# Moving sums of down-projection weights between stages, reordering the last up-projection's splits, and halving the last result's columns

## The chip, the cores and the metric

The kernel runs on one core of a Trainium2 chip. A core has a matrix engine (TensorE, PE in the profile, with its weight loads as PEld), a vector engine (VectorE, DVE), a scalar engine (ScalarE, ACT), a general engine (GpSimd, POOL), and a queue engine (SyncE, SP or SPq) that here issues nearly all transfers. The engines run their own instruction streams in order and wait for each other by semaphores. The metric is the device time of one execution in microseconds (us), as a median over runs.

## The reference, cut to what matters

One layer of a streaming encoder over a prompt of 2048 tokens and 8 short sequences of 16 tokens, in float32. Both go through the same layer with the same weights.

```python
def trunk_layer(x, ...):
    qm, km, vm, om, ip, fp, qa, ka, va = split_in(x @ w_in)
    hm = mlstm_chunkwise(qm, km, vm, logi, logf, C0, n0, m0, mchunk)
    hm = sigmoid(om) * head_norm(hm, g_mlstm_norm)
    ha = windowed attention of rope(qa), rope(ka), va with sinks
    mix = concatenate([hm, ha]) @ w_out
    h = layer_norm(DEEPNORM_ALPHA * x + mix, ln1_g, ln1_b)
    f, conv_rows = conv_ffn(h, conv_prev, w_up, w_conv, b_conv, w_down)
    y = layer_norm(DEEPNORM_ALPHA * h + f, ln2_g, ln2_b)

def conv_ffn(h, conv_prev, w_up, w_conv, b_conv, w_down):
    u = h @ w_up
    ext = concatenate([conv_prev, u], axis=1)
    c = b_conv + sum(ext[:, j:j + T] * w_conv[j] for j in range(CONV_W))
    a, g = split(c, 2)
    return (silu(g) * a) @ w_down, ext[:, -(CONV_W - 1):]
```

The model width is 1024, the input projection 2824 wide, the feed-forward width 2816 (the up-projection twice that, value and gate).

## The kernel before, in words

Tokens are in 17 tiles of 128 (16 of the prompt, one of the 8 short sequences). Three things explain most of the code.

First, every float32 matrix product is made of three products of rounded operands: an operand is split into a rounded high part and the rest (`split`, lines 215 to 218: ScalarE casts, VectorE subtracts), and high x high, high x low and low x high are added in the accumulator. Tiles `w`, `oh`/`ol`, `uw`, `hh`/`hl`, `fu` are such split operands; `wraw` holds the weights as loaded.

Second, each large product is done by seven smaller products instead of eight (Strassen's scheme in Winograd's form), which are numbered s = 1 to 7. They need sums and differences of quarters of the weights and of the tokens, and their results are added up while they are evicted from the accumulator banks A, B and C.

Third, TensorE's order is written by hand; the order on the other engines comes from a scheduler, which places each instruction by when it was issued in the program, its inputs and a few hints (`high_priority`, `issue_after`).

The stages, with their times in the profiled execution: the input projections in four blocks of tokens (b = 0 at 18 to 156 us, b = 1 at 168 to 292, b = 2 at 304 to 460, b = 3 at 472 to 628), woven with the chunkwise recurrence and the attention ("chains"); the output projection (634 to 914); the up-projection (914 to 1847) in three blocks of tokens and 22 column tiles j; the down-projection (1847 to 2312).

What the change touches:

- `i_dense` (line 587 on) walks through blocks b, column groups g (0 to 4; `last` is 4) and products s. Near its end (lines 682 to 687) it calls `d_sums`.
- `d_sums(k, step)` (840) prepares weights of the down-projection ahead of time: for each of 11 indices k it loads two weight tiles (`txy`, step 0, lines 844 and 845), makes four half-width sums on VectorE (step 1, lines 850 to 853) and stores both to `zt` (step 2, lines 855 and 856). The two `txy` tiles take the slots `xr1` and `xr3` that also hold raw tokens for the next block (`x_load`, line 537). Eight of the 11 are done in the input projections and three in the output projection (`o_block`, 1610).
- Gate rows: VectorE works out the logarithms of the gates (`gate_logs`, lines 980 to 997), TensorE multiplies them (`gate_rows`, 1006 and 1007, tile `pgr`).
- Head norm of the recurrence: statistics (1149, 1150), scaling (1152, 1155), small factors (1156 to 1166), scaling again (1168) and a transpose on TensorE (1178, tile `pht`). `ql`, `qh` are the split queries of the attention; `col` (1025) and `emt` (1030) are columns for the recurrence's exponentials.
- `f_ups` (1816): after every product it prepares later ones; with `left` products to go it calls `d_weights` (2009: load and split one unit of weights of the down-projection) and `d_tokens` (2027: split one unit of its tokens, tile `fu`, from `r`). `f_product` (1877) writes the banks; `f_evict` reads them; for s = 5, lines 1906 and 1908 add bank C to a copy of B. At the end `conv_p` and `conv_s` are stored. The last four products of the sequence are s = 5, 2, 3, 4 of the last column tile; s = 4 writes bank C again.
- `f_downs` (2056) runs the down-projection, three blocks, seven products each, six units u of weight rows, up to three token tiles p; line 2087 is its matmul, 512 columns wide. `after` and `add` (2112 to 2118) evict. The very last product is s = 3 of the last block, whose columns p run backwards and end with p = 0. `norm_last` (1540) and `stats` (1550) then do the last layer norm: `bn_stats` per 512 columns (1559), `bn_aggr` (1560), a power on GpSimd (1562), two passes in halves (1545, 1547) and the stores (1548). `st` holds the statistics of the last tile's left half, taken early.

Of the kernel before, what the change touches and what calls it, by code (L numbers as in the profile page):

```python
# [8 lines left out]
F32 = mybir.dt.float32  # L9
# [195 lines left out]
class Prog:  # L205
# [381 lines left out]
    def i_dense(self):  # L587
        nc, a = self.nc, self.a
        nb = len(IBLOCKS)
        last = NG - 1  # L590

        self.next_raw()
        self.x_load(0, 2)
        for _ in range(3):
            self.next_raw()
        self.x_load(0, 4)
        self.single_raw = self.tp.tile([P, KD, P], F32, name="xsr", tag="pth", bufs=2)
        nc.sync.dma_start(self.single_raw, a["xs"])
        self.angles = {}
        self.rope_load(IBLOCKS[0][2], 2)  # L600
        self.rope_load(NPT, 1)
        self.next_split()
        self.x_steps(0, "b12")
        for _ in range(3):
            self.next_split()
        self.x_steps(0, 3)
        self.x_single(1, 2)
        self.x_load(0, 1)
        self.next_raw()
        self.x_load(0, 3)  # L610
        self.x_steps(0, 1)
        self.advance()
        self.x_steps(0, 2, "t3", 7, "t2", 6)
        self.x_single(4)
        self.x_steps(0, "t1", 5, "t4")
        self.sb, self.trans = {}, None

        passages = [{1: ["load"], 7: ["t3", 7], 6: ["t2", 6], 3: [3, "t4"], 4: ["b12", "t1"]},
                    {1: ["load"], 6: ["t3"], 7: [7, "t2"], 5: [6], 3: [3, "t4"], 4: ["b12", "t1"]}]
        sums = 0  # L620
        after = None
        for item in self.items:
            if after:

                after[0] -= 1
                if after[0] == 3:
                    self.logs_of(after[1] - 1)
                if after[0] < 0:
                    self.i_done = after[1]
                    after = None  # L630
            self.chains.hold = item[0] == "t" and item[1] > 0
            if item[0] == "t":
                _, b, ti, e = item
                if ("g", e, 3) not in self.wu:
                    self.advance()
                if b not in self.gates:
                    self.gates[b] = self.tp.tile([P, 5, 8], F32, name="gates", tag="gates", bufs=2)
                ps = self.bank([P, 512], "pg") if ti == 4 else self.ib[ti % 2 * 2]
                yield from self.i_direct(b, ti, e, ps)
                self.i_keys(b, ti, ps)  # L640
                if ti == 1:
                    if b + 1 < nb:
                        self.x_steps(b + 1, 1, 2)
                    else:
                        self.release(4)
                    after = [6, b + 1]
                elif ti == 3 and b or ti == 4:
                    self.release(4)
                    self.x_steps(b, 4)
                    if b:  # L650
                        self.x_steps(b, 5)
                self.advance()
                continue
            _, b, g, s = item
            if item not in self.wu:
                self.advance()
            yield from self.i_product(b, g, s)
            del self.wu[item]
            self.release(2)
            if self.trans and s != 4:  # L660
                self.i_transposes()
            with self.tc.high_priority():
                behind = self.i_after(b, g, s)
            if (b, g, s) == (0, 0, 7):
                self.t_setup()
            if (g, s) == (1, 6):
                self.rope_load(IBLOCKS[b][0], 2)
            if g == last and b + 1 < nb:
                if s == 7:
                    self.rope_load(IBLOCKS[b + 1][2], 2)  # L670
                for x in passages[b > 0].get(s, ()):
                    if x == "load":
                        self.spare = True
                        self.x_load(b + 1, 1, 2, 3, 4)
                    else:
                        self.x_steps(b + 1, x)
            if g == last and b + 1 == nb and s in (7, 5, 2, 3):
                self.x_pair(0, (7, 5, 2, 3).index(s))
            with self.tc.issue_after(behind) if behind and b == 0 else nullcontext():
                self.advance()  # L680

            if b >= nb // 2 and g < last:

                steps = (6, 2, 5) if g == last - 1 else (6, 5, 3)
                if s in steps:
                    self.d_sums(sums, steps.index(s))
                    sums += s == steps[2]
        self.sums = sums
        self.logs_of(nb - 1)
        self.chains.hold = False  # L690
# [846 lines left out]
        self.mix_out(t, 4, mix)  # L1537


    def norm_last(self, y, g, bb, dst, st):  # L1540

        nc, V = self.nc, self.nc.vector
        mv, s = self.stats(y, st)
        for c in (slice(0, 512), slice(512, 1024)):
            V.scalar_tensor_tensor(y[:, c], y[:, c], mv[:, 0:1], g[:, c], op0=ALU.subtract, op1=ALU.mult)
        for c in (slice(0, 512), slice(512, 1024)):
            V.scalar_tensor_tensor(y[:, c], y[:, c], s[:, 0:1], bb[:, c], op0=ALU.mult, op1=ALU.add)
            nc.sync.dma_start(dst[:, c], y[:, c])

    def stats(self, y, st=None):  # L1550
        nc = self.nc
        V = nc.vector
        half = st is not None
        if not half:
            st = self.wp.tile([P, 2, 6], F32, name="lst", tag="lst", bufs=2)
        mv = self.wp.tile([P, 2], F32, name="lmv", tag="lmv", bufs=2)
        s = self.wp.tile([P, 2], F32, name="lsc", tag="lsc", bufs=2)
        for i in range(half, 2):
            V.bn_stats(st[:, i], y[:, i * 512:(i + 1) * 512])  # L1559
        V.bn_aggr(mv, st)  # L1560
        V.tensor_scalar_add(s[:, 1:2], mv[:, 1:2], EPS)
        nc.gpsimd.tensor_tensor(s[:, 0:1], s[:, 1:2], self.mhalf[:, 0:1], op=ALU.pow)
        return mv, s
# [252 lines left out]
    def f_ups(self, n):  # L1816
# [11 lines left out]
        for i, (b, j, s) in enumerate(self.seq):  # L1828
# [25 lines left out]
                self.d_begin()  # L1854

            left = len(self.seq) - i
            if left in (8, 7, 5, 3, 1):
                self.d_weights()
            if left in (9, 8, 7, 6):
                self.d_tokens()  # L1860
        nc.sync.dma_start(self.a["conv_p"], self.prev.rearrange("p v j r -> p (v j) r"))
        nc.sync.dma_start(self.a["conv_s"], self.convs.rearrange("p v j b r -> p (v j) b r"))

# [15 lines left out]
    def f_evict(self, b, j, s):  # L1879
# [22 lines left out]
        elif s == 5:  # L1902
            self.ug = u = half(1)
            u4 = f2.tile([P, 384], F32, name="ub", tag="ub", bufs=1)[:, :h]
            S.copy(u4, B)
            V.tensor_add(u[:, 2 + h:2 + WP], C[:, :m], u4[:, :m])
            if has_s:
                V.tensor_add(sam(u)[:, :, 2:], dec(C), dec(u4))  # L1908
        elif s == 3:
            S.copy(self.uv[:, 2 + h:2 + WP], B[:, :m])  # L1910
            if has_s:
                S.copy(sam(self.uv)[:, :, 2:], dec(B))
        elif s == 4:
            V.tensor_add(self.ug[:, 2:2 + h], C, self.u2[j % 2])  # L1914
# [141 lines left out]
    def f_downs(self):  # L2056
# [17 lines left out]
        nb, nu = len(FBLOCKS), len(DUNITS)  # L2074
        ys, ops = {}, {}
        last_tile = FBLOCKS[-1][0]
        st = self.wp.tile([P, 2, 6], F32, name="st", tag="st", bufs=1)

        def product(s, p, units):
            ps = banks[role[s][2 if p == np_ else p]]  # L2080
            c = slice(p * P, p * P + P)
            for u in units:
                wh, wl, fh, fl = ops[u]
                n = len(DUNITS[u])
                for k in range(n):
                    for i, (l, r) in enumerate(((fh, wh), (fh, wl), (fl, wh))):
                        mm(ps, l[:, k, c], r[:, k], start=s in (1, 4, 7) and u == 0 and k == 0 and i == 0,  # L2087
                           stop=u == nu - 1 and k == n - 1 and i == 2, skip_group_check=True)

        def after(s, p):  # L2090
# [5 lines left out]
            elif s == 2:  # L2096
                add(ta, 0, ps, True)
                if ta == last_tile:
                    V.bn_stats(st[:, 0], ys[ta][:, :512])
            elif s in (4, 6):  # L2100
                add(tb, 0, ps, s == 4)
            elif s == 5 and tb is not None:
# [16 lines left out]

        def finish(t, b, step):  # L2120
            if b == nb - 1 and step == 3:
                self.norm_last(ys[t], *ln2, a["y"][t], st if t == last_tile else None)
                return
            y, (g, bb) = ys[t], ln2
            mv, sc = self.stats(y)
# [8 lines left out]
        for g, (b, s, u) in enumerate(self.dseq):  # L2134
# [16 lines left out]
                    product(s, p, [u])  # L2151
            elif u == 0:
                cols = cols[::-1]
                for p in cols:
                    product(s, p, [u])
            elif u == nu - 1:

                cols = cols[::-1]
                for p in cols:
                    product(s, p, range(1, nu))  # L2160
                    after(s, p)
                    for _ in pending.pop():
                        pass

            for f in pending[:2]:
                if next(f, self) is self:
# [23 lines left out]
```

## Time and profile before

| | us |
|---|---|
| median of 3 runs | 2316.55 |
| the three runs | 2315.92, 2316.55, 2322.16 |
| the profiled execution's own time | 2321.38 |
| its span on the core | 2319.6 |
| mean granted clock of TensorE | 0.995 |
| VectorE busy | 1818.9 (78%) |
| ScalarE busy | 1273.3 (55%) |

The profile is of one execution, and its span is 1.8 us shorter than that execution's own time. A row of the page's groups or of a timeline gives start and length in us, the engine, the line of the code, the operation with the tiles that it writes and reads, their sizes, and in square brackets how long the engine stood idle before it and what it waited for. Matmuls overlap, so a group's length is more than the sum of the distances between starts. A row of the windows gives a stretch, its length, the busy us of the five engines (PE, PEld, DVE, ACT, POOL) with their number of instructions, then the mean granted clock (1.00 is full speed), the DMA share and GB/s.

### The profile page before, as it was taken

To read this page: it belongs to the slowest core of one execution; us is meant where nothing else is said; L and a number is where in the kernel's file an instruction comes from. 1 tells how busy PE (TensorE), PEld (TensorE's weight loads), DVE (VectorE), ACT (ScalarE), POOL (GpSimd) and SP (SyncE) were. 2 spreads that over 40 slices of the span, in tenths; PEclk is the share of its full clock that TensorE was granted. 3 is DMA by queue.
4 is the path that set the end of the run, shared out by engine and by line. 5 is a ranking of instruction groups with operands and counts; after the bars stand their busy time and mean duration, and the time that the engine had idled before them with its cause. 6 is when DMAs were issued, how large, how long until landed. Compare 5 with 4: busy or idle time off the path is not lost. (4 is left out here: it accounts for less than half of the span.)

```text
span 2319.6 us, 39851 instructions
## 1 busy us (share of the span) xinstructions
PE 2287.3 (99%) x14293; PEld 2097.9 (90%) x14293; DVE 1818.9 (78%) x3189; ACT 1273.3 (55%) x2409; POOL 267.8 (12%) x477
## 2 busy tenths in 40 slices
PE   8999999999999999999999999999999999999998
PEld 8999989899977778999999999999999978888876
DVE  7777687787688888998788777678766786895987
ACT  5453466776766665555556555556555544444442
POOL 0001000100011112121102000003111200100200
PEclk9999999999999999999999999999999999999999
DMA  7888999989986767788777888888998776756743
GB/s 270 289 304 294 302 311 329 313 300 327 334 279 225 234 210 271 286 327 310 279 293 270 307 306 307 314 269 283 313 297 265 227 286 205 258 176 218 258 153 109
DMA packets 300166, 632.39 MB, mean 273 GB/s; under 512 B 47868, under 2 KB 141120, under 8 KB 299968
## 3 DMA queue, kind: packets, MB, share of 16 engines
q1 hardware_dynamic: 295296, 616.14, 77.5%
q0 software_dynamic: 3520, 10.56, 1.4%
q10 hardware_dynamic: 1152, 3.15, 0.4%
q8 instruction: 113, 1.85, 0.3%
q14 instruction: 85, 0.70, 0.1%
HBM read 458.11 MB, written 171.64 MB: 271 GB/s over the span
## 5 line engine op out<-in xcount | busy, mean ns | idle before, releaser
L1877 PE MATMUL dps<-hh,uw 128*128 128x384 f32 (+1 forms) x1848 | 478.1, 328 | 2.6 <-DVE u L1908 2.0
L1877 PE MATMUL fup<-hh,uw 128*128 128x384 f32 (+1 forms) x1848 | 478.1, 328 | 0.3 <-ACT ua L1898 0.2
L1877 PEld LDWEIGHTS dps<-hh,uw 128*128 128x128 f32 x1848 | 329.9, 188 | 3.1 <-DVE u L1908 2.3
L1877 PEld LDWEIGHTS fup<-hh,uw 128*128 128x128 f32 x1848 | 330.0, 188 | 0.8 <-ACT ua L1898 0.5
L1934 DVE SCALAR_TENSOR_TENSOR cc<-u,cw,cc 128x768 f32<-128x768 f32 (+1 forms) x264 | 258.2, 979 | 60.9 <-ACT cc L1932 51.8
L1877 PE MATMUL fup<-hl,uw 128*128 128x384 f32 (+1 forms) x924 | 302.5, 327 | 1.8 <-DVE hl L218 1.8
L1877 PE MATMUL dps<-hl,uw 128*128 128x384 f32 (+1 forms) x924 | 302.3, 327 | 0.0
L704 PE MATMUL dps<-w,oh 128*128 128x256 f32 x1344 | 254.9, 284 | 1.2 <-DMA w<-zws 0.7
L217 ACT CAST uw<-wraw 128x1024 fp32r<-128x1024 f32 x126 | 123.1, 979 | 222.8 <-PE dps L2087 120.1
L218 DVE TENSOR_TENSOR w<-wraw,w 128x1024 fp32r<-128x1024 f32 (+2 forms) x167 | 189.3, 1141 | 50.4 <-ACT w L217 45.7
L704 PEld LDWEIGHTS dps<-w,oh 128*128 128x128 f32 x1344 | 210.6, 188 | 12.7 <-issue 8.1
L217 ACT CAST w<-wraw 128x1024 fp32r<-128x1024 f32 (+2 forms) x167 | 163.2, 984 | 102.9 <-PE dps L704 37.3
L218 DVE TENSOR_TENSOR uw<-wraw,uw 128x1024 fp32r<-128x1024 f32 x126 | 142.5, 1132 | 64.3 <-ACT uw L217 64.3
L704 PE MATMUL dps<-w,ol 128*128 128x256 f32 x672 | 187.9, 280 | 0.0
L704 PE MATMUL dps<-oh,w 128*128 128x256 f32 x896 | 172.5, 287 | 6.2 <-ACT mr L1152 3.4
L1877 PEld LDWEIGHTS fup<-hl,uw 128*128 128x128 f32 x924 | 173.5, 188 | 2.5 <-DVE hl L218 2.4
L2087 PE MATMUL fup<-uw,fu 128*128 128x512 f32 x726 | 174.0, 396 | 0.6 <-DVE uw L218 0.6
L1877 PEld LDWEIGHTS dps<-hl,uw 128*128 128x128 f32 x924 | 173.5, 188 | 0.0
L2087 PEld LDWEIGHTS fup<-uw,fu 128*128 128x128 f32 x726 | 136.3, 188 | 34.0 <-DVE uw L218 1.1
L2087 PE MATMUL dps<-uw,fu 128*128 128x512 f32 x660 | 165.3, 396 | 1.1 <-DVE uw L218 1.1
L1932 ACT ACTIVATE cc<-u,cw 128x768 f32<-128x768 f32 (+1 forms) x132 | 132.2, 1001 | 52.6 <-DVE u L1914 26.7
L704 PEld LDWEIGHTS dps<-oh,w 128*128 128x128 f32 x896 | 143.5, 192 | 12.7 <-issue 4.1
(322 smaller groups left out, 4588.6 us busy)
## 6 DMA issues: line engine op xcount, KB each, us to landing
uw<-zw SPq DMA_DIRECT2D x176, 512.0 KB, 5.2
zw<-uw SPq DMA_DIRECT2D x88, 512.0 KB, 3.6
w<-zws SPq DMA_DIRECT2D x72, 512.0 KB, 6.4
wv<-wup SPq DMA_DIRECT2D x66, 512.0 KB, 4.8
wraw<-wi SPq DMA_DIRECT2D x65, 512.0 KB, 5.3
wraw<-zt SPq DMA_DIRECT2D x60, 512.0 KB, 4.3
wraw<-wdn SPq DMA_DIRECT2D x45, 512.0 KB, 4.2
wraw<-wo SPq DMA_DIRECT2D x40, 512.0 KB, 4.7
```

The costliest lines, as they stand in the source:

```text
L217: nc.scalar.copy(hi, src)
L218: nc.vector.tensor_sub(lo, src, hi.bitcast(F32))
L704: mm(o, l, r, start=s in (1, 7) and c == k == i == 0, stop=k == 3 and i == 2, skip_group_check=True)
L1877: mm(ps, l[:, k], r[:, k], start=s in (1, 7) and k == 0 and i == 0, stop=k == 3 and i == 2, skip_group_check=True)
L1932: S.activation(c[:, v], u[:, 2:2 + n], AF.Identity, bias=w[3], scale=w[2])
L1934: V.scalar_tensor_tensor(c[:, v], u[:, i:i + n], w[i], c[:, v], op0=ALU.mult, op1=ALU.add)
L2087: mm(ps, l[:, k, c], r[:, k], start=s in (1, 4, 7) and u == 0 and k == 0 and i == 0, stop=u == nu - 1 and k == n - 1 and i == 2, skip_grou ...
```

## The change

In the input projections the sums are called at other steps and in other blocks:

```diff
-            if b >= nb // 2 and g < last:
-                steps = (6, 2, 5) if g == last - 1 else (6, 5, 3)
-                if s in steps:
-                    self.d_sums(sums, steps.index(s))
-                    sums += s == steps[2]
+            if s in (7, 3, 4) and (b == nb - 1 and g < last or b == nb - 2 and g < last - 1 or b == 1 and g == last - 2):
+                self.d_sums(sums, (7, 3, 4).index(s))
+                sums += s == 4
```

With nb = 4 and last = 4 that was four sums in b = 2 and four in b = 3; it is now one in b = 1 (g = 2), three in b = 2 and four in b = 3. The three in the output projection stay.

In `f_ups` the preparation for the down-projection is issued at other products, and for two of them behind the eviction of s = 5, whose last addition `f_evict` now keeps:

```diff
-            if left in (8, 7, 5, 3, 1):
-                self.d_weights()
-            if left in (9, 8, 7, 6):
-                self.d_tokens()
+            if left in (9, 8, 7):
+                self.d_tokens()
+            if left in (8, 7):
+                self.d_weights()
+            if left in (4, 2):
+                with self.tc.issue_after(self.u4_add):
+                    self.d_weights()
+                    if left == 4:
+                        self.d_tokens()
+            if left == 1:
+                self.d_weights()
...
-            V.tensor_add(u[:, 2 + h:2 + WP], C[:, :m], u4[:, :m])
+            z = V.tensor_add(u[:, 2 + h:2 + WP], C[:, :m], u4[:, :m])
             if has_s:
-                V.tensor_add(sam(u)[:, :, 2:], dec(C), dec(u4))
+                z = V.tensor_add(sam(u)[:, :, 2:], dec(C), dec(u4))
+            self.u4_add = z.ins
```

In `f_downs` the last product's p = 0 is made in two halves of 256 columns. The right half accumulates in another bank, into which ScalarE copies what was there; each half is evicted and gets its own statistics, so `st` has four entries, and `stats` takes none itself when it is given four:

```diff
-        st = self.wp.tile([P, 2, 6], F32, name="st", tag="st", bufs=1)
+        st = self.wp.tile([P, 4, 6], F32, name="st", tag="st", bufs=1)
...
             elif u == 0:
                 cols = cols[::-1]
+                halves = [(slice(i * 256, i * 256 + 256), banks[(role[s][0], 0)[i]][:, :256]) for i in range(2)]
+                S.copy(halves[1][1], banks[role[s][0]][:, 256:])
                 for p in cols:
-                    product(s, p, [u])
+                    for cs, ps in halves if p == 0 else [(slice(0, 512), None)]:
+                        product(s, p, [u], cs, ps)
             elif u == nu - 1:
                 cols = cols[::-1]
-                for p in cols:
+                for p in cols[:-1]:
                     product(s, p, range(1, nu))
                     after(s, p)
                     for _ in pending.pop():
                         pass
+                for i, (cs, ps) in enumerate(halves):
+                    product(s, 0, range(1, nu), cs, ps)
+                    y = ys[last_tile][:, 512 + i * 256:768 + i * 256]
+                    V.scalar_tensor_tensor(y, y, ALPHA, ps, op0=ALU.mult, op1=ALU.add)
+                    V.bn_stats(st[:, 2 + i], y)
+                self.norm_last(ys[last_tile], *ln2, a["y"][last_tile], st)
```

The left half's statistics of that tile (at s = 2) are now taken in two pieces of 256 as well, and `product` takes a column range and a bank. Nothing else in the code changes.

More of the change, by code (lines that the diff above doesn't have):

```diff
@@ L1537, in swa_sample, with norm_last @@
         self.mix_out(t, 4, mix)
-    def norm_last(self, y, g, bb, dst, st):
+    def norm_last(self, y, g, bb, dst, st=None):
         nc, V = self.nc, self.nc.vector
@@ L1557, in stats @@
         s = self.wp.tile([P, 2], F32, name="lsc", tag="lsc", bufs=2)
-        for i in range(half, 2):
-            V.bn_stats(st[:, i], y[:, i * 512:(i + 1) * 512])
+        if st.shape[1] == 2:
+            for i in range(half, 2):
+                V.bn_stats(st[:, i], y[:, i * 512:(i + 1) * 512])
         V.bn_aggr(mv, st)
@@ L2076, in f_downs, with product @@
         last_tile = FBLOCKS[-1][0]
-        st = self.wp.tile([P, 2, 6], F32, name="st", tag="st", bufs=1)
-        def product(s, p, units):
-            ps = banks[role[s][2 if p == np_ else p]]
+        st = self.wp.tile([P, 4, 6], F32, name="st", tag="st", bufs=1)
+        def product(s, p, units, cs=slice(0, 512), ps=None):
+            ps = banks[role[s][2 if p == np_ else p]][:, cs] if ps is None else ps
             c = slice(p * P, p * P + P)
@@ L2086, in product @@
                     for i, (l, r) in enumerate(((fh, wh), (fh, wl), (fl, wh))):
-                        mm(ps, l[:, k, c], r[:, k], start=s in (1, 4, 7) and u == 0 and k == 0 and i == 0,
+                        mm(ps, l[:, k, c], r[:, k, cs], start=s in (1, 4, 7) and u == 0 and k == 0 and i == 0,
                            stop=u == nu - 1 and k == n - 1 and i == 2, skip_group_check=True)
@@ L2098, in after @@
                 if ta == last_tile:
-                    V.bn_stats(st[:, 0], ys[ta][:, :512])
+                    for i in range(2):
+                        V.bn_stats(st[:, i], ys[ta][:, i * 256:i * 256 + 256])
             elif s in (4, 6):
@@ L2121, in finish @@
             if b == nb - 1 and step == 3:
-                self.norm_last(ys[t], *ln2, a["y"][t], st if t == last_tile else None)
+                self.norm_last(ys[t], *ln2, a["y"][t])
                 return
```

## The prediction

> **What bounds the kernel now.** I read the page first: the span and the busy shares.
>
> ```profile
> span 2319.6 us, 39851 instructions
> PE 2287.3 (99%) x14293; PEld 2097.9 (90%) x14293; DVE 1818.9 (78%) x3189; ACT 1273.3 (55%) x2409; POOL 267.8 (12%) x477
> ```
>
> TensorE is busy 2287.3 of 2319.6 us. The change takes no product away and cuts only one into two column halves, so it can touch only the 32 us left: TensorE's waits, what follows its last product, and the clock. So the second view is the list of what TensorE waited for (total us, times, longest), and the third the windows around the longest waits (length, busy us of each engine, then the granted clock PEclk and the DMA share).
>
> ```profile
> PE dps L704 <- ACT mr L1152: 3.4, 1, 3.4
> PE dps L1877 <- DVE u L1908: 2.0, 1, 2.0
> PE ppt L1346 <- ACT sc L1324: 1.5, 1, 1.5
> ```
>
> ```profile
> 328.90:332.38 3.48, 0.04 (x2) 0.01 (x1) 3.33 (x15) 1.68 (x5) 0.00 (x0) 0.78 0.72 239
> 332.38:337.45 5.07, 5.07 (x24) 5.07 (x24) 5.07 (x14) 2.51 (x7) 0.00 (x0) 0.50 1.08 304
> 1842.40:1844.70 2.30, 0.32 (x3) 0.06 (x1) 2.30 (x6) 1.95 (x4) 1.66 (x6) 1.00 0.82 286
> 692.69:696.10 3.41, 3.41 (x11) 2.74 (x10) 2.92 (x9) 2.48 (x7) 1.59 (x2) 0.50 1.00 366
> ```
>
> No single wait is large. The longest, 3.4 us before 332.38, is followed by 5.07 us at a clock of 0.50, which loses half of that, 2.5 us. The 1.5 us wait on the softmax result (L1346, just before the last window, whose 3.41 us are at 0.50 too) also cost half a window, 1.7 us. The 2.0 us wait that ends at 1844.7 had no drop in its own stretch. So a wait costs itself, and a halving on top in some places.
>
> The Trainium skill, "TensorE: Matmul & The Clock Gate", Part 1, says that the clock halves after an idle window of about 3.4 us and that the window is free-running. By that rule only the 3.4 us wait should have halved it; the 1.5 us one did as well, so the trace agrees only in part. By the rule a new wait under 3.4 us costs itself alone; by the 692.69 row it may cost 1.7 us more.
>
> **Part 1a, the sum that moves ahead to the second block.** One of the four sums of the third block (b=2, its group g=3) goes, and one stands in b=1, group g=2. The scheduler places it ahead of the step that issues it, at the front of b=1: its loads take the place, on SyncE's queue, of two token loads (L537) at 167.19 and 169.23, and those and the kva loads go some 15 to 20 us later; they serve the next block, which starts at 304, so this hides. On VectorE the four half-width operations L850 to L853 now stand between L988 and L997, the last step of the gate rows, and one weight split L218 that stood behind L997 stands ahead of it too.
>
> ```profile
> 167.19 0.56 SPq L537 DMA_DIRECT2D xr<-xq  x1
> 169.23 0.43 SPq L537 DMA_DIRECT2D xr<-xq  x1
> ```
>
> Of all the loads of that line, from issue to landing:
>
> ```profile
> DMA to landing us min/median/max: 3.4/4.3/8.0
> ```
>
> ```profile
> 173.59 0.17 DVE L988 TENSOR_SCALAR gl<-gl 128x20 f32<-128x20 f32 x1
> ...
> 177.60 0.18 DVE L997 SCALAR_TENSOR_TENSOR g<-gl,g 128x20 f32<-128x20 f32 x1
> 177.71 3.62 DVE L218 TENSOR_TENSOR w<-wraw,w 128x1024 fp32r<-128x1024 f32 x3
> ```
>
> ```profile
> 179.63 0.27 PE L1006 MATMUL pgr<-ident,g 128*4 128x128 f32 x1
> ```
>
> TensorE multiplies that g at 179.63, at an unchanged place in its order; g ended at 177.78, so the cover is 1.85 us. Ahead of L997 now come four operations of 0.69 us, which follow each other at about 0.61 (the spacing of L850 and its neighbour L1149 below: 327.27 to 327.88), 2.44 us, and one split at 3.62 / 3 less overlap, 1.13. That is 3.57 us against 1.85: TensorE waits a new 1.7 us at about 179.6, with all products of the group behind it. I take 1.7. It is no less than 1.3 (the split alone free), and it grows if a load is late: L851 would start at about 174.8 and needs the load issued at 169.23, 5.6 us before; the token loads at this place took 4.3 us in the middle and 8.0 at most. The weight splits behind are later by the same amount but were ready about 3 us before their products (the split that starts 177.71 ends about 178.9, its product starts 182.2), and TensorE itself is 1.7 later: nothing.
>
> **Part 1b, the sum that goes, and what stays.** The other three sums of b=2 are written at other steps (7,3,4 for 6,5,3), but in the order of the built program they stand exactly where the first three stood, on VectorE and on SyncE alike.
>
> ```profile
> 320.22 0.38 SPq L844 DMA_DIRECT2D txy<-wdn  x1
> ```
>
> ```profile
> 327.27 0.69 DVE L850 TENSOR_TENSOR txy<-txy 128x512 f32<-128x512 f32 x1 [3.32 <-DMA txy<-wdn]
> 327.88 0.29 DVE L1149 BATCH_NORM_STATS2 bst<-pnum 128x6 f32<-128x128 f32 x1
> ...
> 396.44 0.69 DVE L851 TENSOR_TENSOR txy<-txy 128x512 f32<-128x512 f32 x1 [0.74 <-DMA txy<-wdn]
> ```
>
> ```profile
> 409.77 0.91 PE L1178 MATMUL pht<-ident,hn 128*128 128x128 f32 x3 [0.49 <-ACT hn L1168]
> ```
>
> VectorE stood 3.32 us at the second sum's L850 for a load issued at 320.22 that came 7.0 us later; the statistics L1149 are queued behind it, and ScalarE's L1152 behind those; that is the 3.4 us wait of TensorE. Nothing ahead of that load changes, so I leave this wait where it is, at 0 gained; the other bound is the whole of it, 3.4 + 2.5 = 5.9 us, if the load lands as fast as 4.3. The fourth sum, at 394 to 411, goes with its waits on loads and 2.4 us of VectorE: the 0.49 us wait at 409.77 was for a norm whose chain runs through that queue. I take -0.5; between -0.5 and 0.
>
> **Part 1c, the third sum of the last block.** Its loads move on SyncE behind five other loads, its operations on VectorE behind the head norm's chain and two splits.
>
> ```profile
> 518.82 0.69 DVE L850 TENSOR_TENSOR txy<-txy 128x512 f32<-128x512 f32 x1 [1.22 <-DMA txy<-wdn]
> ...
> 521.02 0.16 DVE L1166 TENSOR_TENSOR ms<-ms,mr 128x4 f32<-128x4 f32 x1 [1.23 <-POOL ms L1161]
> ...
> 523.00 0.69 DVE L218 TENSOR_TENSOR ql<-pq,qh 128x512 fp32r<-128x512 f32 x1 [0.49 <-ACT qh L217]
> ```
>
> ```profile
> 523.75 0.66 PE L1178 MATMUL pht<-ident,hn 128*128 128x128 f32 x4 [0.76 <-DVE ql L218]
> ```
>
> The chain L1159, L1160, L1166, ql lay behind the 1.22 us wait and the operation of L850, 1.9 us; it comes that much earlier, so the 0.76 us wait goes: -0.8. Against it: the copy L1025 (col) is now behind L850 to L852, some 1.6 us late with the loads in time, and up to 3 us late with a load of 7 us; ScalarE's exponentials wait for it, but TensorE first needs what follows about 13 us later, at 542, with 2.1 us to spare. Bounds -0.8 and +0.9; I take -0.8.
>
> **Part 2, the end of the up-projection.** Views: the timelines of VectorE and TensorE.
>
> ```profile
> 1841.29 1.22 DVE L218 TENSOR_TENSOR uw<-wraw,uw 128x1024 fp32r<-128x1024 f32 x1
> ...
> 1843.23 0.96 DVE L218 TENSOR_TENSOR fu<-r,fu 128x768 fp32r<-128x768 f32 x1
> 1844.10 0.36 DVE L1906 TENSOR_TENSOR u<-dps,ub 128x192 f32<-128x192 f32 x1
> 1844.37 0.29 DVE L1908 TENSOR_TENSOR u<-dps,ub 128x128 f32<-128x128 f32 x1
> 1844.57 0.56 DVE L218 TENSOR_TENSOR fu<-r,fu 128x384 fp32r<-128x384 f32 x1
> ...
> 1846.78 0.49 DVE L1914 TENSOR_TENSOR u<-dps,ua 128x320 f32<-128x320 f32 x1
> ```
>
> L1908 must read a bank before TensorE may write it with the last product, and it stood behind splits for the down-projection. In the new order two 1.22 us splits (1.13 apart) go behind it, and one fu of 0.96 is replaced by one of 0.56: 2 x 1.13 + 0.4 = 2.7 us earlier. L1908 then ends at 1844.66 - 2.7 = 1842.0, when TensorE has just reached the place (1842.4): the 2.0 us wait goes. The moved splits are done in the stretch to 1849 and their products start at 1853 or later: covered by 4 us; without it each would cost its 1.13. SyncE's conv_p and conv_s stores and one weight load change places with loads that have 10 us of cover.
>
> ```profile
> 1887.99 6.33 PE L2087 MATMUL fup<-uw,fu 128*128 128x512 f32 x26 [0.64 <-DVE uw L218]
> 1894.15 2.94 PE L2087 MATMUL dps<-uw,fu 128*128 128x512 f32 x12
> ```
>
> ```profile
> 1891.92 1.22 DVE L218 TENSOR_TENSOR uw<-wraw,uw 128x1024 fp32r<-128x1024 f32 x1
> 1893.05 1.98 DVE L2116 SCALAR_TENSOR_TENSOR yacc<-yacc,fup 128x512 f32<-128x512 f32 x3
> ```
>
> The split behind the 0.64 us wait at 1887.99 stands some 15 us earlier: another 0.64, in all 2.64. But the split at 1891.92, the first of the step that starts at 1894.15, stood ahead of the three evictions L2116, and in the new order it stands behind them. The last eviction needs the end of the step before (now about 1891.5), then come its 0.61 and the split's 1.22, 1.9 us after that end; only the first product (0.23 us) can go before. So 1.7 us of the 2.64 are given back some 47 us later: -0.9. Bounds: -2.6 if the split is in time, 0 if more is late than this.
>
> **Part 3, the last result.** The last p=0 product is cut into halves of 256 columns.
>
> ```profile
> 2304.80:2312.20 7.40, 7.36 (x32) 5.62 (x30) 5.99 (x11) 0.00 (x0) 1.02 (x2) 1.00 0.33 127
> ```
>
> ```profile
> 172.00:190.00 18.00, 18.00 (x159) 17.85 (x158) 1.00 0.99 343
> ```
>
> ```profile
> 2309.53 1.41 DVE L1547 SCALAR_TENSOR_TENSOR yacc<-yacc,lsc,f_ln_b 128x512 f32<-128x512 f32 x2
> 2312.20 0.69 DVE L2116 SCALAR_TENSOR_TENSOR yacc<-yacc,fht 128x512 f32<-128x512 f32 x1 [1.27 <-PE fht L2087]
> ```
>
> The first row has 32 products 512 wide in 7.36 us, 0.23 each; the second, of L704 alone, 159 of 256 in 18 us, 0.113 each. Two halves cost one whole: 0. The first half ends 27 x 0.113 = 3.1 us before the second (the 27 products behind the first unit), so its eviction and statistics run in VectorE's idle 1.27 us ahead of 2312.20: two operations of about 0.42 (between 0.36 at 192 and 0.49 at 320 columns, L1906 and L1914). Behind the last product stand the second half's two at 0.42 for two at 0.69: -0.54, the surest term; at worst 0. ScalarE's copy of half a bank lies where ScalarE is idle.
>
> The same page of the Trainium skill (Part 1, "Wait — 56ns, not 53.3ns?") gives each warm product a fixed 2.5 ns, which speaks against halving; 33 more products would add an estimated 0.08 us. The two rows show no such cost.
>
> **The sum.** +1.7 - 0.5 - 0.8 - 0.9 - 0.5 = -1.0 us, on the profiled run's own 2321.38 (1.8 more than its span), so 2320.4. That run is 4.8 above the median of 2316.55, and the slowest of the three runs, 2322.16, is 5.6 above: about what the 3.4 us wait with its halving costs, so the median may lack it. Taken off the median: 2315.5. Own range, from the bounds: 2313.4 (all gains, 1.3 for the new wait) to 2319.
>
> **The rivals.** A: the load of the second sum lands in time and the wait at 332 goes, because the moved traffic changes what it meets. For it: it is a 7.0 us landing where 4.3 is usual. Against it: order and slot reuse ahead of it are unchanged. 2315.5 - 5.9 = 2309.6. B, the slower side: at the new sum in b=1 VectorE waits at L851 for its load, as it does at 327.27, with L997 and L1006 behind it. It decides from a landing over 5.6 us; at 7.0 or a little above, the wait on TensorE becomes about 3.5 us, and the clock halves as at 332.38, 2.5 us: 6.0 in place of 1.7, +3.3 in all, so 2319.9. For it: the DMA share is 0.99 there (172.00 row). Against it: the load replaces another of the same size at the same place. A wait of 1.7 alone, with a halved window (1.7), would give 2317.2. C: the down-projection's late split gives all of part 2 back, or the up-projection's last wait moves to another operand: 2316.4.
>
> **How the numbers follow.** A measurement of this kernel can tell about 0.3%, 6.9 us, from no change: faster is below 2309.6, slower above 2323.5. Forecast 0.44, A 0.22, B 0.24, C 0.10. Of A two thirds lie below the bound, since a clock window more or less decides (0.15, with 0.02 of the forecast 0.17); of B half reach the upper one, if a second window halves or the other late terms add (0.12, with 0.02 from C and the slowest runs 0.14); the rest, 0.69, is no change. The range, to A on one side and past B on the other: 2308 to 2322.
>
> **What would show it.** Right: a TensorE wait of about 1.7 us on L997's g near 179.6; the 3.4 us wait still there near 332; none at 409.8, 523.8, 1844.7 and 1888; a new one of about 1.7 us on a uw split near 1892; and from the last product to the end of the span half a microsecond less. Wrong: no wait at 179.6, which would mean that the gate rows have more cover than I counted; or a new wait over 3 us anywhere in the blocks b=1 to b=3.

## The result and the profile after

| | kernel before | changed kernel |
|---|---|---|
| median, us | 2317.99 (22 runs) | 2322.73 (22 runs) |
| lowest to highest, us | 2313.71 to 2323.13 | 2320.20 to 2330.12 |
| ratio to before | | 1.0024, 95% interval 1.0017 to 1.0031 |
| profiled execution, own time / span, us | 2321.38 / 2319.6 | 2320.77 / 2318.9 |

The change makes the kernel slower by 0.24%, 5.6 us by the ratio (3.9 to 7.2); the forecast was 1 us faster, 2315.5, with 2308 to 2322 as range. (The median of before, here of 22 runs, is 1.4 us above that of the three runs from which the forecast started.) The two profiled executions do not show the loss: by chance that of before is one of its slow ones (3.4 us above its median), that of the changed kernel one of its fast ones (2 us below). Stretches at half clock took 11.3 us of the first span and 4.7 of the second (span times one less the mean clock, 0.9951 and 0.9980). So the spans can't be subtracted; they have to be compared place by place.

First the waits. The list of TensorE's waits in the changed kernel (total us, times, longest):

```profile
PE dps L2095 <- DVE uw L218: 2.8, 2, 1.7
PE dps L702 <- ACT mr L1150: 2.4, 1, 2.4
PE dps L327 <- DVE zero L322: 2.0, 1, 2.0
PE dps L728 <- ACT oh L565: 1.6, 1, 1.6
PE ppt L1344 <- ACT sc L1322: 1.5, 1, 1.5
```

The lines are a few off those of before. The wait of 2.0 us on `u` (before's L1908) is gone, and no new one as long stands in the list but that of 1.7 us on a `uw` split, which the prediction had. VectorE at the second sum of b=2, in the timeline, still stands for its load, and TensorE's wait behind it is still there, 2.4 us in place of 3.4:

```profile
327.77 0.69 DVE L848 TENSOR_TENSOR txy<-txy 128x512 f32<-128x512 f32 x1 [2.37 <-DMA txy<-wdn]
```

The end of the up-projection and the first steps of the down-projection, in TensorE's and in VectorE's timeline:

```profile
1844.79 0.31 PE L1884 MATMUL dps<-hl,uw 128*128 128x320 f32 x1
...
1895.50 2.83 PE L2095 MATMUL dps<-uw,fu 128*128 128x512 f32 x11 [1.68 <-DVE uw L218]
```

```profile
1892.25 2.06 DVE L2125 SCALAR_TENSOR_TENSOR yacc<-yacc,fup 128x512 f32<-128x512 f32 x3
1894.23 1.22 DVE L218 TENSOR_TENSOR uw<-wraw,uw 128x1024 fp32r<-128x1024 f32 x1
```

The split now stands behind the three evictions, and one product after the step's start TensorE waits 1.68 us for it. And the tail, VectorE's timeline:

```profile
2310.55 0.42 DVE L2180 SCALAR_TENSOR_TENSOR yacc<-yacc,fht 128x256 f32<-128x256 f32 x1
2311.00 0.43 DVE L2181 BATCH_NORM_STATS2 st<-yacc 128x6 f32<-128x256 f32 x1
2311.95 0.42 DVE L2180 SCALAR_TENSOR_TENSOR yacc<-yacc,fup 128x256 f32<-128x256 f32 x1 [0.51 <-PE fup L2095]
2312.40 0.43 DVE L2181 BATCH_NORM_STATS2 st<-yacc 128x6 f32<-128x256 f32 x1
```

The first half's two operations run before the second half is done, and each takes 0.42 to 0.43 us. So far the profile is much as forecast. The loss is where TensorE does not wait at all. Near 179 us, where the prediction has a wait of 1.7 us, TensorE's timeline of the changed kernel has none:

```profile
177.75 0.43 PE L702 MATMUL dps<-oh,w 128*128 128x256 f32 x2
178.01 0.30 PE L702 MATMUL dps<-ol,w 128*128 128x256 f32 x1
178.15 0.43 PE L702 MATMUL dps<-oh,w 128*128 128x256 f32 x2
178.41 0.30 PE L702 MATMUL dps<-ol,w 128*128 128x256 f32 x1
...
179.57 0.27 PE L1004 MATMUL pgr<-ident,g 128*4 128x128 f32 x1
```

Three matmuls of 256 columns take 0.40 us here (177.75 to 178.15), 133 ns each. In the kernel before, the same matmuls of the same product take 0.34 us (178.15 to 178.49), 113 each:

```profile
178.15 0.39 PE L704 MATMUL dps<-oh,w 128*128 128x256 f32 x2
178.38 0.28 PE L704 MATMUL dps<-ol,w 128*128 128x256 f32 x1
178.49 0.39 PE L704 MATMUL dps<-oh,w 128*128 128x256 f32 x2
178.72 0.28 PE L704 MATMUL dps<-ol,w 128*128 128x256 f32 x1
```

No idle time stands between them and the granted clock is 1.00. The same product, the same engine, the same clock, but a lower pace. This product is an extreme one: over all matmuls that stream tokens the loss is some 4 ns each, as a table below shows. The windows (length, busy us and number of PE and PEld, clock, DMA share, GB/s) from 184 to 190 us, matmuls of that line alone, before and after:

```profile
184.00:190.00 6.00, 6.00 (x56) 6.00 (x55) 1.00 1.00 333
```

```profile
184.00:190.00 6.00, 6.00 (x53) 6.00 (x52) 1.00 1.03 373
```

Busy time is 6.00 of 6.00 in both; only the count differs, 56 against 53. (It takes in matmuls that are under way at the window's edges; 53 and 50 start inside it, one in 113 and one in 120 ns.) What changed for these matmuls? Not their order. But `st` grew from 48 bytes in each partition (in a slot of 64) to 96, and it lies in a pool at the bottom of the memory: in the built program every tile of the pools behind it (tokens `oh`, `ol`, and in the up-projection `hh2` to `hh5` and the last two weight slots) stands 32 bytes further on, while the eight weight slots ahead of it stay. Theory A is that these addresses cost the time; its rival, theory S, that the moved instructions do.

### The profile page after: what moved, and what is told of

It reads as the page before. It is cut to its first block, busy times and chain, and to the rows that moved or that the text cites. A ratio compares the mean times of both kernels' runs of the same rounds, so it can differ in the third digit from the quotient of the medians.

```text
span 2318.9 us, 39919 instructions
## 1 busy us (share of the span) xinstructions
PE 2289.0 (99%) x14326; PEld 2102.4 (91%) x14326; DVE 1820.1 (78%) x3192; ACT 1273.4 (55%) x2410; POOL 257.2 (11%) x477
## 3 DMA queue, kind: packets, MB, share of 16 engines
q8 instruction: 113, 1.85, 0.3%
## 5 line engine op out<-in xcount | busy, mean ns | idle before, releaser
L702 PE MATMUL dps<-oh,w 128*128 128x256 f32 x896 | 175.0, 288 | 5.1 <-ACT mr L1150 2.4
L2095 PE MATMUL fup<-uw,fu 128*128 128x512 f32 (+1 forms) x759 | 177.6, 390 | 0.3 <-ACT fht L2103 0.3
L2095 PEld LDWEIGHTS dps<-uw,fu 128*128 128x128 f32 x660 | 123.9, 188 | 32.8 <-DVE uw L218 3.6
```

Source lines behind the costliest of these rows:

```text
L702: mm(o, l, r, start=s in (1, 7) and c == k == i == 0, stop=k == 3 and i == 2, skip_group_check=True)
L2095: mm(ps, l[:, k, c], r[:, k, cs], start=s in (1, 4, 7) and u == 0 and k == 0 and i == 0, stop=u == nu - 1 and k == n - 1 and i == 2, skip_ ...
```

## The experiments

All times are ratios to the kernel before, measured beside it on the same chip, with 95% intervals; us are the ratio times the median of before (2317). Where only padding differs, the order of instructions on every engine is the same as in the kernel that it is built from.

**Addresses alone (b32).** The kernel before, with the long `st` and nothing else:

```diff
-        st = self.wp.tile([P, 2, 6], F32, name="st", tag="st", bufs=1)
+        st = self.wp.tile([P, 4, 6], F32, name="st", tag="st", bufs=1)[:, :2]
```

> The kernel before, with st made twice as long (96 instead of 48 bytes a partition) and its second half unused: instruction order on all engines unchanged, every tile of the pools behind it stands 32 bytes further on. Theory A (addresses: the matmuls that read the tokens oh, ol as the moving operand lose pace when these start 32 bytes off a 64-byte step; 119.5 instead of 115.7 ns in the two traces, some 1230 of them, 4.9 us, and about 1 us on others): slower than before by 4 to 7 us, with no new wait of TensorE. Theory S (the order of instructions costs the time): as before, within 1 us.

Measured 1.0033 (1.0023 to 1.0044): 7.6 us slower, with no part of the change in it but the size of a tile. Theory A had 4 to 7 us, theory S none. Its window at the same place, as above:

```profile
184.00:190.00 6.00, 6.00 (x52) 6.00 (x51) 1.00 0.96 355
```

and its list of waits still has the 2.0 us of before:

```profile
PE dps L1877 <- DVE u L1908: 2.0, 1, 2.0
PE dps L704 <- ACT mr L1152: 1.9, 1, 1.9
```

**The change with the addresses of before (a0).** `st` in a pool of the down-projection, where no matmul operand lies behind it:

```diff
-        st = self.wp.tile([P, 4, 6], F32, name="st", tag="st", bufs=1)
+        self.wp.tile([P, 2, 6], F32, name="st", tag="st", bufs=1)
+        st = f2.tile([P, 32], F32, name="st4", tag="st4", bufs=1)[:, :24].rearrange("p (a b) -> p a b", b=6)
```

> The changed kernel with its order unchanged, but the long st in a pool of the down-projection, so that all operands of matmuls lie where they lay before the change. Theory A: faster than before by 1 to 3 us (what the three parts gain by themselves, forecast -1.0), that is 5 to 8 us faster than the changed kernel; the matmuls with moving oh, ol at 113 to 116 ns again. Theory S: like the changed kernel, 4 to 5 us slower than before.

Measured 1.0001 (0.9991 to 1.0012): the whole loss is gone, and with it nothing is won either; 0.2 us, between -2.1 and +2.8. A window of six us in its products:

```profile
182.00:188.00 6.00, 6.00 (x56) 6.00 (x55) 1.00 1.03 383
```

The pace is back (the window is two us earlier because other work follows from 189 us on), and now the forecast wait appears. TensorE's and VectorE's timelines of a0:

```profile
176.72 0.28 PE L702 MATMUL dps<-oh,w 128*128 128x256 f32 x1
178.00 0.27 PE L1004 MATMUL pgr<-ident,g 128*4 128x128 f32 x1 [1.00 <-DVE g L995]
```

```profile
175.15 1.22 DVE L218 TENSOR_TENSOR w<-wraw,w 128x1024 fp32r<-128x1024 f32 x1
176.28 1.24 DVE L992 SCALAR_TENSOR_TENSOR gl<-gl,gl 128x20 f32<-128x20 f32 x6
...
177.77 0.18 DVE L995 SCALAR_TENSOR_TENSOR g<-gl,g 128x20 f32<-128x20 f32 x1
```

In the changed kernel the last matmul ahead of that point starts at 179.30, 2.6 us later than here, and `g` ends at 179.51, only 1.6 us later: nearly nothing is left of the wait. That the slower matmuls alone bring this is not shown.

**Shifts by 64 and by 128 bytes (a64, b128).** The changed kernel with `st` padded to 128 bytes (64 more than the slot of before), and the kernel before with 192 (128 more); the line of `st` becomes:

```diff
+        st = self.wp.tile([P, 32], F32, name="st", tag="st", bufs=1)[:, :24].rearrange("p (a b) -> p a b", b=6)
...
+        st = self.wp.tile([P, 48], F32, name="st", tag="st", bufs=1)[:, :12].rearrange("p (a b) -> p a b", b=6)
```

> The changed kernel with st padded to 128 bytes, so that all later tiles lie 64 bytes further on than before, on a 64-byte step again but on the other half of a 128-byte step. Theory A, if the 64-byte step is what counts: like a0, within 1 us. Theory A, if the 128-byte step counts: between a0 and the changed kernel or like the changed one. Theory S: like the changed kernel.

> The kernel before, order unchanged, all tiles behind st 128 bytes further on. If the place within a 128-byte step is what counts: as before, within 2 us, moving oh, ol at 115 to 116 ns. If the distance to something fixed counts in larger steps, or if any other place is worse: slower by 4 to 8 us, like the shifts by 32 and 64 bytes.

Measured: a64 1.0032 (1.0021 to 1.0043), b128 1.0005 (0.9994 to 1.0016). A 64-byte step does not help, a 128-byte step restores. b128 at the place of the windows above:

```profile
184.00:190.00 6.00, 6.00 (x56) 6.00 (x55) 1.00 1.01 363
```

**Own place or distance (bw64).** The weight slots alone moved by 64, everything behind by 128:

```diff
             self.wp = es.enter_context(self.pool("wsb"))
+            self.wp.tile([P, 16], F32, name="wpad", tag="wpad", bufs=1)
...
+        st = self.wp.tile([P, 32], F32, name="st", tag="st", bufs=1)[:, :12].rearrange("p (a b) -> p a b", b=6)
```

> The kernel before, order unchanged, the eight weight slots 64 bytes further on (from 64 to 0 within a 128-byte step), all behind them 128 bytes (their place within the step unchanged, oh and ol at 0). Theory H1 (each operand is read fastest when it starts on a 128-byte step): faster by 3 to 8 us, since the 1877 matmuls of 256 columns that stream w would go from 117.2 to about 115 ns or less and those that stream oh, ol would stay. Theory H2 (what counts is the distance between the streamed and the loaded operand within the step; 64 bytes apart is best, as it is in the kernel before, 0 or 32 apart is slow): slower by 4 to 9 us, the matmuls that stream oh, ol at 119 ns instead of 115.5 and those that stream w at 118.7 instead of 117.2.

Measured 1.0025 (1.0016 to 1.0035), 5.8 us slower: now weights and tokens both start on a 128-byte step, and that is bad. H1 falls, H2 stands. A window of six us in its products:

```profile
182.00:188.00 6.00, 6.00 (x53) 6.00 (x52) 1.00 0.81 275
```

The traces of both kernels, of b32, a0, a64, b128 and bw64, and of p1, t1 and t2 below give a table. For each matmul I took the time from its start to the next one's on the same line (times more than 1.4 of the usual one, that is waits and stretches at half clock, left out), and from the built program the place of the two operands; shown is the mean in ns by the distance between streamed and loaded operand within a 128-byte step:

| matmul | 0 bytes | 32 | 64 | 96 |
|---|---|---|---|---|
| tokens streamed, 256 columns | 119.1 | | 115.4 | 119.4 |
| weights streamed, 256 columns | 118.7 | 117.9 | 117.2 | |
| up-projection tokens, 384 columns | 174.9 | 175.0 | 173.9 | 175.3 |
| up-projection tokens, 320 columns | 146.7 | 146.7 | 146.6 | 146.7 |
| down-projection weights, 512 columns | 232.6 | 233.4 | 231.0 | 233.4 |

At 256, 384 and 512 columns 64 bytes apart is the fastest, by 0.6 to 3.5%; at 320 columns the distance makes no difference. Nor is it all that counts: at 64 the 512-column matmuls took 229 ns in the changed kernel and b32, with the loaded `fu` at 96 within the step, and 231.3 to 231.6 in t1 and t2, with it at 0. The kernel before has 64 in its input projections, and 96 or 32 in its down-projection.

**Where the loss lies (bi32).** The shift of b32, undone behind the projections by a pad of 96 bytes ahead of the last two weight slots:

```diff
+        st = self.wp.tile([P, 4, 6], F32, name="st", tag="st", bufs=1)[:, :2]
...
             self.wx, wxcm = enter("wx2sb")
+            self.wx.tile([P, 24], F32, name="wxpad", tag="wxpad", bufs=1)
```

> The kernel before, order unchanged, with the 32-byte shift of b32 in the input and output projections only; in the up- and down-projection the places within the 128-byte step are those of before. H2: slower by 4 to 7 us (1232 matmuls with streamed oh, ol x 3.9 ns = 4.8, 1877 with streamed w x 0.8 = 1.4, waits take some of it), the pace of the later stages as before; b32's remainder, 1 to 3 us, is the later stages'. If the later stages carry the loss: within 2 us of before.

Measured 1.0030 (1.0019 to 1.0042), 7 us: nearly all of b32's loss is in the input and output projections. What is left for the later stages can't be told apart from nothing. In b32's trace two effects cancel there: the 384-column matmuls take 1.5 us more than before in all, and the 512-column ones 1.8 us less, since the last two weight slots came to a distance of 64.

**The distance put right elsewhere (t1, t2, t2b).** On a0, a pad at the end of the right-hand pool moves `fu`, `hh1`, `hh6`, `hh7` from 96 to 0 (t1); pads also bring the last two weight slots to 64 (t2). t2b is t2's pads in the kernel before, without any of the three parts.

```diff
         self.in_down = True
+        self.fp.tile([P, 24], F32, name="fpad", tag="fpad", bufs=1)
...
             self.wx, wxcm = enter("wx2sb")
+            self.wx.tile([P, 16], F32, name="wxpad", tag="wxpad", bufs=1)
...
             self.f2, f2cm = enter("f2sb")
+            self.f2.tile([P, 16], F32, name="f2pad", tag="f2pad", bufs=1)
```

> The changed kernel with addresses as in a0, and the tiles of the right-hand pool 96 bytes lower, so that fu (loaded in the down-projection) and hh1, hh6, hh7 stand at 0 instead of 96 within a 128-byte step. H2: fu is now 64 bytes from eight of ten weight slots: the 512-column matmuls at about 229 instead of 233.3 ns for these, 1580 x 4 ns, 5 to 7 us faster than a0 and than before, and 0 to 1 us more in the up-projection. H1: fu and hh start on a 128-byte step, the streamed weights still at 64: faster by 0 to 4 us. If neither holds there: as a0, within 2 us.

> As t1, and the last two weight slots (wx2) at 64 instead of 0 within the step, so that all ten are 64 bytes from fu and from hh1, 2, 3, 5, 6, 7. H2: another 1 to 2 us faster than t1 (390 matmuls of 512 columns and some 700 of 384). H1: 0 to 2 us slower than t1.

> The kernel before, none of the three parts, with the two shifts of t2 (fu, hh1, hh6, hh7 at 0 and the last two weight slots at 64 within the step). H2: 4 to 8 us faster than before, as t2 within 2 us, since the three parts together are worth nothing that shows. If t2's gain came from the parts together with the shifts: within 2 us of before.

Measured: t1 0.9980 (0.9969 to 0.9990), t2 0.9969 (0.9958 to 0.9980), t2b 0.9978 (0.9964 to 0.9992). t2, at a median of 2309.99 us, beats both kernels: 7.2 us under the kernel before, with the three parts in; t2b, at 2310.47, shows that the pads alone bring it. The chain that ended last has a stretch of 198 matmuls of 512 columns (start, length in us) in each kernel, here of before and of t2:

```profile
2009.83 46.17 PE fup L2087 x198
```

```profile
2006.97 45.87 PE fup L2099 x198
```

0.30 us in 46. By the mean over all 512-column matmuls t2 runs at 231.6 ns and a0 at 233.3, 3.4 us over 1972; less than the 229 that I had expected from a few weights at another place, so t1 came out at the lower end or under its range. More of t2's gain is in the 384-column matmuls that stream a high part, 173.7 against 174.5 in some 2400, 1.9 us. That is 5.3 of the 7.2 us measured (4.6 to 9.7).

**The parts one by one (p1, p2, p3),** each alone in the kernel before, with the addresses of before. The edits are the three parts of the diff.

> The kernel before with part 1 alone (the sums moved between the blocks), st and addresses as before. Theory A: between -2 and +1 us. Theory S, with the sums as its cause: slower by 4 to 5 us, with a wait of TensorE near 179 us or lost pace at 170 to 190 us.

> The kernel before with part 2 alone, addresses unchanged. Prediction's terms: the waits of 2.0 us near 1844 and of 0.64 us near 1888 gone, a new one of 1.7 us on a uw split at the start of the step after, near 1892; time -0.9 us, that is no difference that shows. If the moved splits reach further: a second new wait between 1850 and 1890.

> The kernel before with part 3 alone, the long st kept out of the way so that addresses are unchanged. Prediction's term: from the end of the last matmul to the end of the span 0.5 us less (6.9 in place of 7.45), the two half products as long as one whole; time -0.5 us, that is no difference that shows. If narrow matmuls cost a fixed time each: 0.08 us or more longer in the last product.

Measured: p1 1.0002 (0.9993 to 1.0012), p2 0.9998 (0.9986 to 1.0010), p3 1.0008 (0.9998 to 1.0018): none differs from nothing. In p1's list of waits, and in p2's:

```profile
PE pgr L1003 <- DVE g L994: 0.7, 1, 0.7
```

```profile
PE dps L2096 <- DVE uw L218: 2.8, 2, 1.7
```

p1 has the wait on the gate rows, at 0.7 us. p2 has the late split (1.7, the other 1.1 is that near the end, as before), and no wait on `u`. In p3 the last products and VectorE's tail:

```profile
2304.57 3.35 PE L2090 MATMUL fup<-uw,fu 128*128 128x256 f32 x27
```

```profile
2307.95 0.42 DVE L2175 SCALAR_TENSOR_TENSOR yacc<-yacc,fup 128x256 f32<-128x256 f32 x1 [0.57 <-PE fup L2090]
2308.41 0.43 DVE L2176 BATCH_NORM_STATS2 st<-yacc 128x6 f32<-128x256 f32 x1
```

From the end of that last product to the end of the span are 7.0 us (2307.9 to 2314.9); before, 7.45 (2312.16 to 2319.61).

With p1, p2 and p3 at nothing, theory S has fallen. The profiles, one execution of each kernel, say the same: TensorE's busy time, less what the granted clock took of the span (worked out as above), is 2276.0 us before and 2276.1 to 2278.4 in p1, p2, p3, a0 and b128; 2282.1 to 2284.6 in the changed kernel, b32, a64, bi32 and bw64; 2269.7 to 2271.9 in t1, t2 and t2b. These groups go by the addresses, whatever the order.

## Why the prediction was wrong

The step that failed is the costing of part 3, and under it the first step of all, that the change "can touch only the 32 us left" beside TensorE's busy time. Part 3 counted operations (the halves, the evictions, the statistics) and was put between 0 and -0.54. The longer `st` stands in the diff, but the prediction gave it no cost at all: it never asked what lies behind that tile in memory. The runs put +7.6 us in that place (b32, 5.3 to 10.2; between a0 and the changed kernel the ratios differ by 5.3 us), more than all gains together. None of the rivals was of this kind either: A, B and C are all waits, and this loss has no wait in it. The first view of the prediction had the sign of what it overlooked: with TensorE busy 99% of the span, the 2287 us of busy time are no fixed amount, and 0.3% of pace, 6.9 us, is more than any wait on the list. The prediction itself quoted 113 ns for one stretch (159 matmuls in 18 us, of which 157 start in it) and took it for the cost of 256 columns; the means of the same line in that kernel are 115.7 (tokens streamed) and 117.1 (weights streamed).

The other terms, by the runs in which the addresses are those of before:

- **Part 1a, +1.7.** The mechanism was right, the size not: 0.7 us in p1, 1.0 in a0, 0.4 in t1 and t2. The cover of 1.85 us was read from one profile; in other kernels with the order of before it is 1.8 to 3.9 (p3 and bw64), and before is near the low end. The bound of 1.3 was too high as well: with the split free, 2.44 - 1.85 leaves 0.6. In the changed kernel there is no such wait, which the prediction named as a sign that the gate rows have more cover than it counted. The load was in time in all runs, so rival B fell.
- **Part 1b.** The wait near 332 stayed, as forecast, at 1.9 to 3.2 us in p1, a0, a64, b32 and the changed kernel, and rival A fell. It varies from run to run with the load: VectorE stood 3.32 us for it before and 2.37 in the changed kernel. The 0.49 us wait near 410 is gone in p1, a0 and the changed kernel, as forecast; but it is missing from p2, b128 and bw64 too, which have the order of before, so this shows little.
- **Part 1c, -0.8.** The wait at 523.8 is gone in p1, a0 and the changed kernel (in b128 and bw64 as well), and one of 0.6 to 0.75 us on the head norm stands some 30 us later (556.9 in the changed kernel; in no kernel with the order of before). The prediction followed what moved for 13 us and not for one group more. The three terms of part 1 summed to +0.4; p1 gave +0.5 (-1.6 to +2.8).
- **Part 2, -0.9.** All three waits came as worked out: 2.0 and 0.64 gone, 1.68 new, so most is given back at the start of the second step after. The wait of 2.0 is worth more in some executions: in b32 and bw64 3.4 us at a clock of 0.50 follow it (from 1849.5 and 1844.8), another 1.7 us, and in before none. In a0 and in the changed kernel one of 0.3 to 0.5 us on ScalarE's copy near 1869 comes on top (2.0 in t2); p2 has none. The time of p2 shows no difference.
- **Part 3 without the longer st, -0.54.** 0.45 us off the tail in p3, a0 and the changed kernel; the 0.42 us for 256 columns was right, and a wider aggregate (0.26 for 0.21) takes a little. The second half's 27 matmuls took 3.35 us with the last one's own length, 0.12 each: the two halves cost no more than a whole product.
- **The sum.** -1.0 was forecast for what a0 measures as +0.2 (-2.1 to +2.8). Without the addresses the forecast would have held, in part by luck: the wait of part 1a came out too large and the one near 557 was not counted.
- **The profile it started from.** Its 4.8 us above the median were put down to the 3.4 us wait near 332 and the halving behind it. But a wait there and 3.4 us at 0.50 behind it are in p1 too (2.9 us), which ran 4.7 us faster. What p1 lacks are 6.8 us at half clock from 10.0 and 3.4 from 40.7, 5.1 us lost.

The clock does not explain the loss: it is 0.998 in the changed kernel's profile and 0.995 in that of before.

Two things stay open. The runs show that the pace goes with the distance of the operands within a 128-byte step, but not why, nor why 320 columns are spared, nor whether it is the weights of the same matmul or of the next one, loaded meanwhile, that matter. And the table has means: the 133 ns near 178 us are one product with one pair of slots, and what makes that pair worse than others at the same distance was not tried.

## What to carry to other kernels

A tile that grows moves every tile behind it: before costing an edit, compare the addresses of matmul operands in both built programs, and when an experiment is to show the effect of an order, hold the addresses. Where TensorE is busy all the time, read its pace (matmuls per window, or distance of starts) beside its waits; a busy share of 99% can hide several us either way. In this kernel pads of 64 and 96 bytes were worth more than the three reorderings together.

## What the runs showed of the hardware

- The pace of back-to-back float32 (rounded) matmuls depends on where their operands start: with streamed and loaded operand 64 bytes apart within a 128-byte step, 256 columns with the tokens streamed took 115.4 ns, otherwise 119.1 to 119.4; with the weights streamed 117.2, otherwise 117.9 to 118.7. Moving one operand by 128 bytes changes nothing that shows (b128), moving one by 32 or 64 costs up to 3.5% of the pace. The Trainium skill, "TensorE: Matmul & The Clock Gate", Part 1, "Wait — 56ns, not 53.3ns?", has for bfloat16 matmuls a warm pace of columns / 2.4 GHz + 2.5 ns, an estimate of 109 ns for 256 columns, without addresses; the traces here lie above it, from 113 to 133 ns.
- It is a steady property of the addresses, not of the run: b32 and the changed kernel, with different orders, both show 2417 matmuls of 384 columns with a high part streamed at 174.9 ns, and before, p1 and a0 at 174.5 to 174.6.
- No wait and no granted clock names it: at full clock (1.00) and 6.00 of 6.00 us busy, 56 matmuls became 52 to 53 in the count of a window. It shows in such counts and in the times from start to start.
- A wait of about 2 us can halve the granted clock or not: the same one was followed by 3.4 us at 0.50 in b32 and bw64 and by none in before.
